# Rotating sixteen rows of each dilated head in one packed tile instead of in two full tiles

## The chip, the cores and the metric

The kernel runs on one core of one Trainium2 chip. The metric is the device time of one execution in microseconds (us), lower is better. A core has five engines that each run their own instruction list in order: PE (TensorE, matrix products and transposes), DVE (VectorE, elementwise work), ACT (ScalarE, activations and copies), POOL (GpSimd) and SP (SyncE, which here issues all transfers). They are tied together by semaphores; data moved by DMA is announced by a semaphore as well.

## The reference

Two layers of an encoder, applied to 256 and 512 tokens (768 together, called T) of width 1024. Each layer adds three things to its input: a mixer with three groups of heads (A dilated, B recurrent, C grouped-query), cross-attention into 256 memory tokens, and a gated feed-forward block with a short convolution. The change touches only the A group, four heads of 64 dimensions whose queries and keys get a rotary embedding in the first 16 of the 64 dimensions:

```python
def rotate(x, cos, sin):
    half = x.shape[-1] // 2
    x1, x2 = x[..., :half], x[..., half:]
    return concatenate([x1 * cos - x2 * sin, x1 * sin + x2 * cos], axis=-1)

def partial_rope(x, rope):            # ROPE_DIMS = 64 // 4 = 16
    return concatenate([rotate(x[..., :16], *rope), x[..., 16:]], axis=-1)
```

The rotated queries and keys then go through a masked attention whose result is the mixture of three (window, dilation) branches. Everything is in 32-bit floats and must come out at that accuracy.

## The kernel before

Activations lie transposed: the feature dimension is on the 128 partitions, the 768 tokens lie along a row. A product of full accuracy is made from halves: each operand is split into a high part and a low remainder (`split`, line 325, one ACT instruction and one DVE instruction), and three matrix products are summed (lines 213 to 215 for projections, 378 and 379 for scores, 400 and 401 for values).

The mixer of a layer is a list of stages, of which two at a time are interleaved by `ahead` (line 353). The call sites are lines 886 to 902: the projection of the first pair of A heads runs beside the second attention of group B (`b_attn(1)`), the projection of the second pair beside the attention of the first pair (`a_attn(0)`). So there are four calls of `a_proj` in the program, two in each layer; they are called places 1 and 2 (layer 0) and places 3 and 4 (layer 1). Nothing is ordered by hand: the tile framework gives each engine its list by priorities and a simulated timeline, so a change of instructions in one stage can shift rows of the stages beside it.

`a_proj` (line 792) projects queries (j=0) and keys (j=1) of two heads into one tile `z2` of 128 partitions by 1536; the two heads stand on partitions 0 to 63 and 64 to 127, so the rows that rotate are partitions 0 to 15 and 64 to 79. POOL clears a second tile `zs2` of the same size (line 798), and four transfers (lines 803 and 804) copy the rows of `z2` into it with their halves swapped. Then three DVE operations run over all 128 partitions for j=0 and three for j=1, `zs*sa`, `z*ca` and `z+zs`; on the rows that don't rotate the tables hold 1 and 0. All elementwise calls go through the helper `tt` (line 158), so they all carry that line. The result is split (the two halves of the queries and of the keys), and `stacks` (line 682) builds from the halves, by transfers of line 365, the operands of the scores: four of 64x768 for the queries, and four of 64x1536 (384 KB) for the keys, called the key stacks below. The score products of the next stage wait for them. Line 943 of the profile of the changed kernel is line 935 here: from line 798 on the numbers shift by up to 8.

Buffers come from two arenas, `arena_f` (plain) and `arena_r` (operands of matrix products); a tile that is freed is handed out again, and whoever gets it waits for the old tile's readers.

Of the kernel before, what the change touches and what calls it, by code (L numbers as in the profile page):

```python
# [13 lines left out]
ALU = mybir.AluOpType  # L14
# [16 lines left out]
T = 768  # L31
# [77 lines left out]
def trunk_kernel(ctx, tc, xT, memT, w_in, w_out, w_xq, w_xkv, w_xo, w_up, w_dn, w_dnt, par, fin_g, cst, fmk, tabs,  # L109
                 out_p, out_s):  # L110
    nc = tc.nc
    V, A, G, PE, SY = nc.vector, nc.scalar, nc.gpsimd, nc.tensor, nc.sync
# [14 lines left out]
    af = Arena(f_all, F_COLS)  # L127
# [3 lines left out]
    ft = lambda n=T: af.tile(n)  # L131
# [25 lines left out]
    def tt(out, a, b, op):  # L157
        V.tensor_tensor(out, a, b, op=op)  # L158
# [81 lines left out]
    def proj(src, xh, xl, evac, streams=STREAMS, sub="", chunks=None):  # L240
        chunks = chunks or wload8(src, sub)
        for c0, n in streams:
            ps = ps_tile(n)
            mm_chunks(ps[:, :n], chunks, xh, xl, c0, n)
            evac(ps[:, :n], c0, n)
# [79 lines left out]
    def split(src, hi, lo, n, scale=None, sub="sp"):  # L325
        hi_op(pick("h" + sub, "A"), hi[:, :n], src[:, :n], scale)
        if scale is None:
            tt(lo[:, :n], src[:, :n], hi.bitcast(F32)[:, :n], ALU.subtract)
        else:
            stt(lo[:, :n], src[:, :n], scale, hi.bitcast(F32)[:, :n], ALU.mult, ALU.subtract)  # L330
# [187 lines left out]
    def mixers(l, xt, x_dram, stats):  # L518
# [7 lines left out]
        def ev_to(z, name):  # L526
            return ev_scaled(z, rbc, name)

        def load_tab(j):
            t = ft()  # L530
            SY.dma_start(out=t, in_=tabs[j])
            return t
# [47 lines left out]
        C = {}  # L580
# [38 lines left out]
        def v_proj(t):  # L619
            zv = ft()  # L620
            proj(w_in[l, t], xh, xl, ev_to(zv, "v%d" % t), sub="w_v%d" % t)
            vv = [rtl(), rtl()]
            v_tokens(zv, 6, [tok(v) for v in vv], "v%d" % t)
            af.free(zv)
            return vv
# [56 lines left out]
        def stacks(qq, kk):  # L682
            out = []
            qf, kf = qq.bitcast(F32), kk.bitcast(F32)
            for e in range(2):
                r = slice(64 * e, 64 * e + 64)
                qs, K = rtl(), rtl(2 * T)
                load_stack(qs, [(0, qf[r, :T]), (64, qf[r, T:])])
                load_stack(K, [(0, kf[r]), (64, kf[r])])
                out.append((qs, K))  # L690
            ar.free(qq, kk)
            return out
# [99 lines left out]
        def a_proj(pg):  # L792
            if pg == 0:
                C["ca"], C["sa"] = load_tab(2), load_tab(3)
                C["fm"] = ft(896)
                SY.dma_start(out=C["fm"], in_=fmk)
            z2, zs2 = ft(2 * T), ft(2 * T)
            G.memset(zs2, 0.0)
            for j in range(2):
                proj(w_in[l, 2 * j + pg], xh, xl, ev_to(z2[:, j * T:(j + 1) * T], "a%d%d" % (pg, j)), sub="w_a%d%d" % (pg, j))  # L800
            for e in range(2):
                r = 64 * e
                SY.dma_start(out=zs2[r:r + 8], in_=z2[r + 8:r + 16])
                SY.dma_start(out=zs2[r + 8:r + 16], in_=z2[r:r + 8])
            parts = []
            for j in range(2):
                z, zs = z2[:, j * T:(j + 1) * T], zs2[:, j * T:(j + 1) * T]
                tt(zs, zs, C["sa"], ALU.mult)
                tt(z, z, C["ca"], ALU.mult)
                tt(z, z, zs, ALU.add)  # L810
                hl = rtl(2 * T)
                if j:
                    split(z, hl[:, :T], hl[:, T:], T, sub="a_sp%d" % pg)
                else:
                    split(z, hl[:, :T], hl[:, T:], T, scale=0.125, sub="saq%d" % pg)
                parts.append(hl)
            af.free(z2, zs2)
            if pg == 1:
                af.free(C["ca"], C["sa"])
            sts = stacks(*parts)  # L820
            return sts, v_proj(4 + pg)
# [65 lines left out]
        sb0 = ahead(lambda: b_proj(0), lambda: c_attn(1, qc1), "1")  # L887
        sb1 = ahead(lambda: b_proj(1), lambda: b_attn(0, sb0), "2")
        sa0 = ahead(lambda: a_proj(0), lambda: b_attn(1, sb1), "3")
        def fa():  # L890
            r = a_proj(1)
            return r
# [421 lines left out]
def _layout(i):  # L1314
# [24 lines left out]
    r = np.arange  # L1339
# [39 lines left out]
    p = np.arange(128)  # L1379
# [31 lines left out]
    both = lambda t: np.concatenate([t[:, :256], t], 1)  # L1411
    tabs[0], tabs[1] = both(np.cos(ang)), both(np.sin(ang))
    inva = (f(500000.0) ** (-np.arange(0, 16, 2, dtype=f) / f(16))).astype(f)
    d = p % 64
    ang = (pos[None].astype(f) * inva[d % 8][:, None]).astype(f)
    tabs[2] = both(np.where((d < 16)[:, None], np.cos(ang), 1))
    tabs[3] = both(np.where((d < 8)[:, None], -np.sin(ang), np.where((d < 16)[:, None], np.sin(ang), 0)))
# [26 lines left out]
```

## Time and profile before

| | us |
|---|---|
| median of 3 runs (2142.23 to 2144.77) | 2144.53 |
| the profiled execution | 2145.01 |
| its span in the trace | 2143.2 |
| PE busy | 2003.8 (93%) |
| DVE busy | 1841.7 (86%) |
| ACT busy | 1061.7 (50%) |
| POOL busy | 7.8 |

PE is busy for 93% of the span. That is an average: in the feed-forward blocks it never idles, in the mixers it does. A row of the timeline names the start, the duration, the engine, the line and the tiles (result first), and in brackets how long the engine stood idle before it and what ended the wait. `SPq` rows are the issuing of transfers. PEclk is the granted TensorE clock as a share of its upper level, so 0.50 is the lower one, 1.2 of 2.4 GHz.

### The profile page before, as it was taken

Reading aid. Unit: us, or ns where it says so; the run is one execution under the profiler, and the core shown is the slowest. Engines: PE = TensorE matmul, PEld = TensorE weight load, DVE = VectorE, ACT = ScalarE, POOL = GpSimd, SP = SyncE. Lnnn points to the kernel's source line nnn. Section 1 sums busy time; section 2 is a strip of 40 time slices with the busy share of each in tenths; the row PEclk is TensorE's granted clock in tenths of the full one; section 3 lists DMA queues with packets and bytes.
Section 4 is the critical chain, followed back from the end, with each engine's and each line's share of the span. In section 5 each row is a group of like instructions: output and inputs, shape, how many; then the busy total and the mean of one; then the engine's idle time right before and its main releaser. Section 6 shows DMA issues by size and latency. Waiting matters only on the chain.

```text
span 2143.2 us, 31059 instructions
## 1 busy us (share of the span) xinstructions
PE 2003.8 (93%) x11280; PEld 1782.8 (83%) x11280; DVE 1841.7 (86%) x3822; ACT 1061.7 (50%) x2119; POOL 7.8 (0%) x32
## 2 busy tenths in 40 slices
PE   7989989998899999999999897999988999999997
PEld 5878768787789999999888775777877999999995
DVE  8787887867999999999977868778779999999998
ACT  4257767547533333333534667565665333333342
POOL 0000000000000000000000000000000000000000
PEclk8989989999999999999999998999999999999998
DMA  5433335342132212212254314343421222222202
GB/s 179 138 82 101 96 89 124 110 132 80 50 90 79 67 62 72 74 63 88 65 179 117 92 44 107 99 111 123 124 64 56 83 70 69 70 69 70 69 30 79
DMA packets 62953, 190.94 MB, mean 89 GB/s; under 512 B 8072, under 2 KB 11400, under 8 KB 62032
## 3 DMA queue, kind: packets, MB, share of 16 engines
q1 hardware_dynamic: 62800, 188.96, 30.1%
q8 instruction: 89, 1.46, 0.3%
q14 instruction: 64, 0.52, 0.1%
HBM read 145.97 MB, written 10.71 MB: 73 GB/s over the span
## 4 chain that ended last, share of the span: by engine, by line
PE 74%; DVE 16%; ACT 4%; DMA 3%; issue 2%; SPq 1%; POOL 0%; DVEq 0%; ACTq 0%
PE rps L1105 8%; PE rps L1107 8%; PE rps L1106 8%; PE rps L1148 5%; PE rps L1149 5%; PE rps L1150 5%; PE prS L213 4%; PE prS L214 4%; PE prS L215 4%; DVE arena_f L158 4%; PE t L392 3%; PE prP L213 2%; PE prP L214 2%; PE prP L215 2%; DVE arena_r L158 2%
## 5 line engine op out<-in xcount | busy, mean ns | idle before, releaser
L158 DVE TENSOR_TENSOR arena_f<-arena_f 128x512 f32<-128x512 f32 (+2 forms) x373 | 265.6, 728 | 27.7 <-DMA arena_f<-arena_f 15.2
L183 ACT CAST wh<-arena_f 128x512 fp32r<-128x512 f32 x266 | 162.2, 621 | 253.0 <-PE rps L1106 212.8
L183 ACT CAST wh<-wr 128x512 fp32r<-128x512 f32 x260 | 159.4, 620 | 236.3 <-PE rps L1106 98.9
L158 DVE TENSOR_TENSOR xall<-rps,xall 128x512 f32<-128x512 f32 (+1 forms) x384 | 197.9, 549 | 14.1 <-PE rps L1150 6.9
L1148 PE MATMUL rps<-arena_r,wh 128*128 128x512 f32 (+1 forms) x608 | 202.6, 339 | 3.4 <-DVE xall L158 3.2
L158 DVE TENSOR_TENSOR wl<-wr,wh 128x512 fp32r<-128x512 f32 x264 | 179.5, 683 | 29.5 <-ACT wh L183 27.9
L1105 PE MATMUL rps<-xha,wh 128*128 128x384 f32 x608 | 203.9, 335 | 0.5 <-ACT wh L183 0.4
L1106 PE MATMUL rps<-xla,wh 128*128 128x384 f32 x608 | 203.4, 335 | 0.0
L1149 PE MATMUL rps<-arena_r,wh 128*128 128x512 f32 (+1 forms) x608 | 201.2, 338 | 0.0
L1107 PE MATMUL rps<-xha,wl 128*128 128x384 f32 x608 | 199.2, 334 | 0.0
L213 PE MATMUL prS<-xha,wh 128*128 128x512 f32 x480 | 188.8, 397 | 3.1 <-DVE arena_f L158 1.0
L215 PE MATMUL prS<-xha,wl 128*128 128x512 f32 x480 | 189.1, 396 | 1.5 <-DVE wl L158 1.5
L214 PE MATMUL prS<-xla,wh 128*128 128x512 f32 x480 | 189.9, 396 | 0.0
L158 DVE TENSOR_TENSOR wl<-arena_f,wh 128x512 fp32r<-128x512 f32 x266 | 179.2, 684 | 1.5 <-ACT wh L183 1.3
L1150 PE MATMUL rps<-arena_r,wl 128*128 128x512 f32 (+1 forms) x608 | 178.3, 339 | 0.0
L158 DVE TENSOR_TENSOR arena_f<-rps,arena_f 128x384 f32<-128x384 f32 x266 | 143.6, 552 | 28.2 <-PE rps L1107 26.0
L1105 PE MATMUL rps<-arena_r,wh 128*128 128x384 f32 x456 | 152.8, 335 | 0.0
L1106 PE MATMUL rps<-arena_r,wh 128*128 128x384 f32 x456 | 152.3, 334 | 0.0
L158 DVE TENSOR_TENSOR arena_r<-t,arena_r 128x512 fp32r<-128x512 f32 x184 | 124.9, 683 | 27.8 <-ACT arena_r L183 24.4
L213 PE MATMUL prP<-xha,wh 128*128 128x256 f32 x480 | 138.9, 289 | 9.8 <-DVE xall L158 5.9
L1107 PE MATMUL rps<-arena_r,wl 128*128 128x384 f32 x456 | 146.4, 334 | 0.0
L392 PE MATMUL t<-cs,arena_f 128*128 128x128 f32 x736 | 125.6, 291 | 13.9 <-DVE arena_r L158 7.5
(235 smaller groups left out, 5004.7 us busy)
## 6 DMA issues: line engine op xcount, KB each, us to landing
arena_f<-in_w_up SPq DMA_DIRECT2D x76, 512.0 KB, 3.6
wr<-in_w_in SPq DMA_DIRECT2D x42, 512.0 KB, 3.6
wr<-in_w_dn SPq DMA_DIRECT2D x40, 512.0 KB, 3.7
wr<-in_w_out SPq DMA_DIRECT2D x32, 512.0 KB, 5.2
arena_r<-arena_r SPq DMA_DIRECT2D x32, 384.0 KB, 6.7
arena_r<-arena_r SPq DMA_DIRECT2D x48, 192.0 KB, 4.0
xall<-in_xT SPq DMA_DIRECT2D x8, 768.0 KB, 8.7
arena_r<-arena_r SPq DMA_DIRECT2D x64, 96.0 KB, 2.2
```

What stands on the lines that cost most here:

```text
L158: V.tensor_tensor(out, a, b, op=op)
L183: A.copy(out, a)
L213: PE.matmul(ps, h[:, j], xh[i][:, c0:c0 + n], start=i == 0, stop=False)
L214: PE.matmul(ps, h[:, j], xl[i][:, c0:c0 + n], start=False, stop=False)
L215: PE.matmul(ps, lo[:, j], xh[i][:, c0:c0 + n], start=False, stop=i == tot - 1)
L392: PE.transpose(t[:, j * n + i * 128:j * n + (i + 1) * 128], ptiles[i][:, (kb + j) * 128:(kb + j + 1) * 128], ident)
L1105: PE.matmul(ps, h[:, k], x[k], start=k == 0, stop=False)
L1106: PE.matmul(ps, h[:, k], x[4 + k], start=False, stop=False)
L1107: PE.matmul(ps, lo[:, k], x[k], start=False, stop=k == 3)
L1148: PE.matmul(ps, h[:, m], hh[i][:, c], start=k == 0 and not tail, stop=False)
L1149: PE.matmul(ps, h[:, m], hlo[i][:, c], start=False, stop=False)
L1150: PE.matmul(ps, lo[:, m], hh[i][:, c], start=False, stop=i == b - 1)
```

## The change

`zs2` goes. Two tiles of 128x768 take its place, `zc` for the rows as they are and `zs` for the rows with their halves swapped. The 16 rotating rows of each of the two heads, of queries and of keys, are packed into four blocks of `zc` and `zs`, at partitions 0, 32, 64 and 96, by 12 transfers (lines 806 to 808). The three DVE operations run once on the packed tiles. Four transfers (line 815) put the rotated rows back into `z2`. The tables repeat every 32 partitions instead of every 64.

```diff
-            z2, zs2 = ft(2 * T), ft(2 * T)
-            G.memset(zs2, 0.0)
+            z2, zc, zs = ft(2 * T), ft(), ft()
+            G.memset(zc, 0.0)
+            G.memset(zs, 0.0)
             for j in range(2):
                 proj(w_in[l, 2 * j + pg], xh, xl, ev_to(z2[:, j * T:(j + 1) * T], "a%d%d" % (pg, j)), sub="w_a%d%d" % (pg, j))
-            for e in range(2):
-                r = 64 * e
-                SY.dma_start(out=zs2[r:r + 8], in_=z2[r + 8:r + 16])
-                SY.dma_start(out=zs2[r + 8:r + 16], in_=z2[r:r + 8])
+            for j in range(2):
+                for e in range(2):
+                    r, b = 64 * e, 64 * j + 32 * e
+                    z = z2[r:r + 16, j * T:(j + 1) * T]
+                    SY.dma_start(out=zc[b:b + 16], in_=z)
+                    SY.dma_start(out=zs[b:b + 8], in_=z[8:16])
+                    SY.dma_start(out=zs[b + 8:b + 16], in_=z[0:8])
+            tt(zs, zs, C["sa"], ALU.mult)
+            tt(zc, zc, C["ca"], ALU.mult)
+            tt(zc, zc, zs, ALU.add)
+            for j in range(2):
+                for e in range(2):
+                    b = 64 * j + 32 * e
+                    SY.dma_start(out=z2[64 * e:64 * e + 16, j * T:(j + 1) * T], in_=zc[b:b + 16])
             parts = []
             for j in range(2):
-                z, zs = z2[:, j * T:(j + 1) * T], zs2[:, j * T:(j + 1) * T]
-                tt(zs, zs, C["sa"], ALU.mult)
-                tt(z, z, C["ca"], ALU.mult)
-                tt(z, z, zs, ALU.add)
+                z = z2[:, j * T:(j + 1) * T]
                 hl = rtl(2 * T)
...
-            af.free(z2, zs2)
+            af.free(z2, zc, zs)
...
-    d = p % 64
+    d = p % 32
```

The lists of the engines move with it, in the mixers of both layers; the feed-forward blocks keep their order. Below are rows of the lists before and after; they tell an order and no times.

DVE at place 3, before. `L769` is the masked softmax work of `b_attn(1)`; `prP` and `prS` rows take the projections out of the accumulators, and the row `x4` is the rotation's first four operations:

```order
2235 L158 TENSOR_TENSOR arena_f<-prP,rbc 128x256
2236 L158 TENSOR_TENSOR wl<-wr,wh 128x512
2237 L158 TENSOR_TENSOR arena_f<-arena_f 128x768 x4
2238 L158 TENSOR_TENSOR xall<-yps,xall 64x512
2239 L769 ISA arena_f,dn<-s,arena_f 128x512
2240 L769 ISA dn 128x1
```

DVE at place 3, after. Row 2210 is the eviction that the last six packing transfers wait for, row 2227 the first of the three rotation operations:

```order
2210 L158 TENSOR_TENSOR arena_f<-prP,rbc 128x256
2211 L158 TENSOR_TENSOR wl<-wr,wh 128x512
2212 L158 TENSOR_TENSOR arena_r<-t,arena_r 128x512 x2
2213 L769 ISA arena_f,dn<-s,arena_f 128x384
2214 L769 ISA dn 128x1
2215 L158 TENSOR_TENSOR arena_f<-prS,rbc 128x512
2216 L158 TENSOR_TENSOR xall<-yps,xall 64x512
2217 L769 ISA arena_f,dn<-s,arena_f 128x384
```

Eight rows further down in the same list the rotation begins:

```order
2225 L769 ISA arena_f,dn<-s,arena_f 128x128
2226 L769 ISA dn 128x1
2227 L158 TENSOR_TENSOR arena_f<-arena_f 128x768
2228 L158 TENSOR_TENSOR arena_r<-t,arena_r 128x512
2229 L769 ISA arena_f,dn<-s,arena_f 128x256
```

The rotation stood right behind the last eviction; now sixteen rows of other work stand between the two.

SP at place 4 (layer 1, second pair), before. The `64x1536` rows are the key stacks, `scr_k` and `scr_v` rows load the operands of the cross-attention:

```order
185 L177 DMA wr<-in_w_out 128x1024
186 L365 DMA arena_r<-arena_r 64x768 x4
187 L365 DMA arena_r<-arena_r 64x1536 x2
188 L365 DMA arena_r<-scr_k 64x2048 x2
189 L365 DMA arena_r<-arena_r 64x1536 x2
190 L935 DMA arena_r<-scr_v 128x1024
```

SP at place 4, after, from the last packing transfer on:

```order
218 L808 DMA arena_f<-arena_f 8x768
219 L815 DMA arena_f<-arena_f 16x768 x4
220 L365 DMA arena_r<-arena_r 64x768 x2
221 L177 DMA wr<-in_w_out 128x1024
222 L365 DMA arena_r<-arena_r 64x768 x2
223 L365 DMA arena_r<-scr_k 64x2048 x2
224 L365 DMA arena_r<-arena_r 64x1536 x4
225 L943 DMA arena_r<-scr_v 128x1024
```

All four key stacks now stand behind the two loads from `scr_k`, where two stood ahead of them. At place 2 one `scr_k` load (512 KB) now stands ahead of the four stacks, where none did.

SP at place 1, after: `L806` to `L808` are the packing transfers, `L815` the way back.

```order
46 L806 DMA arena_f<-arena_f 16x768 x2
47 L177 DMA wr<-in_w_in 128x1024 x2
48 L806 DMA arena_f<-arena_f 16x768
49 L807 DMA arena_f<-arena_f 8x768
50 L808 DMA arena_f<-arena_f 8x768
51 L807 DMA arena_f<-arena_f 8x768
52 L808 DMA arena_f<-arena_f 8x768
53 L807 DMA arena_f<-arena_f 8x768
54 L808 DMA arena_f<-arena_f 8x768
55 L806 DMA arena_f<-arena_f 16x768
56 L807 DMA arena_f<-arena_f 8x768
57 L808 DMA arena_f<-arena_f 8x768
```

Before, the four swaps (two of line 803, two of line 804) stood here; now ten transfers stand behind the last weight loads of this pair, of which the eighth (row 55) completes `zc` and the tenth completes `zs`.

## Rows read from the trace of the kernel before

**Rows 1.** The page: busy times, and the costliest group of DVE.

```profile
PE 2003.8 (93%) x11280; PEld 1782.8 (83%) x11280; DVE 1841.7 (86%) x3822; ACT 1061.7 (50%) x2119; POOL 7.8 (0%) x32
...
L158 DVE TENSOR_TENSOR arena_f<-arena_f 128x512 f32<-128x512 f32 (+2 forms) x373 | 265.6, 728 | 27.7 <-DMA arena_f<-arena_f 15.2
```

**Rows 2.** Windows: both layers' places (first, last) and a feed-forward stretch; first row names columns.

```profile
core 0: us, PE busy (x) PEld busy (x) DVE busy (x) ACT busy (x) POOL busy (x), PEclk, DMA share, GB/s
300.00:400.00 100.00, 92.97 (x531) 77.32 (x529) 85.30 (x248) 70.65 (x169) 1.38 (x1) 0.97 0.45 113
700.00:1000.00 300.00, 300.00 (x1724) 286.13 (x1723) 286.03 (x484) 112.29 (x171) 0.00 (x0) 1.00 0.22 69
1300.00:1400.00 100.00, 85.04 (x444) 68.94 (x443) 75.17 (x265) 60.32 (x150) 2.77 (x2) 0.86 0.40 105
```

**Rows 3.** Timeline of DVE: the rotation at places 1 to 4.

```profile
300.79 3.56 DVE L158 TENSOR_TENSOR arena_f<-arena_f 128x768 f32<-128x768 f32 x4 [1.98 <-DMA arena_f<-arena_f]
...
346.44 3.57 DVE L158 TENSOR_TENSOR arena_f<-arena_f 128x768 f32<-128x768 f32 x4 [4.20 <-DMA arena_f<-arena_f]
...
1349.90 3.56 DVE L158 TENSOR_TENSOR arena_f<-arena_f 128x768 f32<-128x768 f32 x4 [4.63 <-DMA arena_f<-arena_f]
...
1395.70 3.56 DVE L158 TENSOR_TENSOR arena_f<-arena_f 128x768 f32<-128x768 f32 x4 [4.41 <-DMA arena_f<-arena_f]
...
1400.71 0.94 DVE L158 TENSOR_TENSOR arena_f<-arena_f 128x768 f32<-128x768 f32 x1
```

**Rows 4.** Timeline of SP: first and last of four swapping transfers at place 1; first at place 3.

```profile
295.70 0.73 SPq L803 DMA_DIRECT2D arena_f<-arena_f  x1
...
297.90 0.62 SPq L804 DMA_DIRECT2D arena_f<-arena_f  x1
...
1344.74 0.72 SPq L803 DMA_DIRECT2D arena_f<-arena_f  x1
```

**Rows 5.** Windows: the stretches behind places 1 and 3.

```profile
315.00:320.00 5.00, 1.70 (x5) 0.95 (x6) 5.00 (x26) 3.78 (x12) 0.00 (x0) 0.77 0.72 160
320.00:325.00 5.00, 4.70 (x18) 3.42 (x17) 5.00 (x32) 5.00 (x15) 0.00 (x0) 0.54 0.86 198
...
1365.00:1370.00 5.00, 2.19 (x8) 1.00 (x6) 5.00 (x25) 4.21 (x13) 0.00 (x0) 0.91 0.89 186
1370.00:1375.00 5.00, 4.89 (x18) 3.90 (x17) 5.00 (x31) 4.66 (x14) 0.00 (x0) 0.50 0.63 153
```

**Rows 6.** Timeline of PE: its longest wait behind place 1.

```profile
317.07 0.47 PE L378 MATMUL s<-arena_r 128*128 128x512 f32 x1 [2.14 <-DVE dn L158]
```

**Rows 7.** Timeline of PE: the waits for the key stacks, places 2 and 4.

```profile
365.99 0.47 PE L378 MATMUL s<-arena_r 128*128 128x512 f32 x1 [1.45 <-DMA arena_r<-arena_r]
...
1427.05 0.74 PE L378 MATMUL s<-arena_r 128*128 128x512 f32 x1 [2.69 <-DMA arena_r<-arena_r]
```

**Rows 8.** Chain of waits: from the last issue of swaps at place 1, of stacks later.

```profile
297.90 2.81 DMA arena_f<-arena_f
...
359.87 5.98 DMA arena_r<-arena_r
...
1417.60 9.21 DMA arena_r<-arena_r
```

**Rows 9.** Windows: the transfers at place 2, and the low clock at place 4.

```profile
355.00:360.00 5.00, 5.00 (x29) 4.21 (x28) 4.97 (x11) 4.95 (x11) 0.00 (x0) 1.00 0.89 240
360.00:365.00 5.00, 4.54 (x29) 3.81 (x27) 4.17 (x10) 3.11 (x8) 0.00 (x0) 1.00 0.94 198
...
1425.00:1430.00 5.00, 2.95 (x9) 2.50 (x10) 2.07 (x5) 2.68 (x6) 0.00 (x0) 0.71 0.40 122
```

**Rows 10.** Timeline of DVE: the two splits of place 2 (DVE's part of each).

```profile
356.29 0.95 DVE L161 SCALAR_TENSOR_TENSOR arena_r<-arena_f,arena_r 128x768 fp32r<-128x768 f32 x1
...
358.38 0.95 DVE L158 TENSOR_TENSOR arena_r<-arena_f,arena_r 128x768 fp32r<-128x768 f32 x1
```

## The prediction

> **What bounds the kernel now.** I read the page first, then the windows, then the timeline of each engine at the four places, then the chain of waits. The page says PE 93% busy and DVE 86%, and its costliest group of DVE, the arena operations, has 27.7 us of idle time before it, of which 15.2 us end with a transfer within the arena [rows 1]. The windows show that 93% is an average of two regimes: in a feed-forward stretch PE is busy for 300.00 of 300 us with DVE at 286.03, while around the A heads of layer 0 PE has 92.97 of 100 and in layer 1 85.04 of 100, and the clock there is below the upper level for part of the time [rows 2]. So only the mixers have something to give.
>
> The 15.2 us are the four waits for the swapping transfers: 1.98, 4.20, 4.63 and 4.41 us [rows 3]. They are DVE's idle time, not PE's. PE's losses lie elsewhere, in two forms. Behind places 1 and 3 DVE has a backlog, is 100% busy for ten microseconds, and PE starves: it is busy for 1.70 and 2.19 of 5 us, and in the five that follow it runs at a granted clock of 0.54 and 0.50, that is near or at the 1.2 GHz level, after having stood idle [rows 5]; its longest single wait there, 2.14 us, ends with DVE [rows 6]. At places 2 and 4 PE waits 1.45 and 2.69 us for the key stacks [rows 7].
>
> **The change part by part.**
>
> *Removed.* Three of six DVE operations per place. Four in a row take 3.56 us, 0.89 each; single ones 0.94 [rows 3]. So 2.7 us per place, 10.7 in all. POOL clears the same number of bytes; POOL is hardly used.
>
> *Added on SP.* 16 transfers per place instead of four. Issuing one takes 0.62 to 0.73 us [rows 4], I take 0.68, and from the last issue to DVE's start it is 2.9 us (297.90 to 300.79, rows 3 and 4; the chain books 2.81 of it as the transfer, rows 8). Before, the chain is 5.1 us (295.70 to 300.79). With k transfers left after the last eviction it is (k-1) x 0.68 + 2.9.
>
> The Trainium skill, in "DMA: Bandwidth & Descriptors", section "Rules for kernel authors", speaks against the change: it says to merge small transfers, since below 64 KB one pays mostly overhead; the change cuts 48 KB swaps into pieces of 24 and 48 KB. Its section "Anatomy of one DMA" (fitted for another issuing path) gives about 2 us plus the bytes at 436 GB/s, an estimate of 2.1 us for 48 KB; the chain of waits shows 2.81, and the trace decides. With 2.1 the sum would come out about 1.4 us lower per place, for the two hops.
>
> *Added hop.* The split waits for rotated rows that come back by DMA: 0.68 + 2.9 = 3.6 us from the last operation for the queries, 3 x 0.68 + 2.9 = 4.9 for the keys. Whatever is queued behind the waiting row on DVE waits too: the softmax of the B heads and the evictions that PE's next products need.
>
> *Place 1.* The first operation needs the eighth transfer after the eviction: 7 x 0.68 + 2.9 = 7.7 us. In the new order some 20 rows stand in between, about 4.2 us by their like in the trace (five of 128x512 at 0.73, the page's group mean, rows 1; the others short); the wait is 3.5 us against 1.98, so +1.5. Three operations go, -2.7. The hop of 3.6 us is covered by about 2.8 us, +0.8. DVE comes out 0.4 us ahead. I take 0. From below, the most that can come back is what PE loses there: 3.3 + 0.3 us idle, and 4.70 x 0.46 + 1.70 x 0.23 = 2.6 us of clock [rows 5], 6.2. From above, with the cover late as well, 1.5 + 2.8 = 4.3 us.
>
> *Place 3.* All twelve stand behind the last eviction: 11 x 0.68 + 2.9 = 10.4 us. Sixteen rows stand in between, about 5.5 us by the same means; the wait of 4.9 us is nearly the 4.63 of before, but 5.5 us of softmax and evictions have run in the meantime instead of adding to the backlog. The hop is covered by about 4 us of rows; the splits themselves come later than before, by 1 to 3 us, since more work stands ahead of them. I take -2, most of what the removed operations give. Bounds: -5.5 (idle 2.8 + 0.1, clock 4.89 x 0.50 + 2.19 x 0.09 = 2.6, rows 5) and +4 (the hop uncovered).
>
> *Place 2.* Six transfers follow the eviction: 6.3 us, 1.2 more than before, and 2.5 us of softmax now stands in the gap that was 4.20 us. Before, the splits started 9.85 and 11.94 us after the rotation did [rows 3, 10]. Now: rotation 1.2 later, three operations instead of six, then about 6 us of other rows that hide the 4.9 us hop; the splits come out 1 to 2 us earlier. Against it stands one more 512 KB load ahead of the stacks; at the 198 to 240 GB/s of that stretch [rows 9] it takes 2.2 to 2.6 us. The stacks land 1 us later; PE already waits for them, so +1. Bounds: -1.45 (the wait of rows 7 gone) and +3.
>
> *Place 4.* The first six transfers run during the second projection, six follow: 6.3 us. There DVE has the slack to hide the hop. Before, the last two stacks were issued at 1417.60 - 0.5, long after the split, and took 9.21 us [rows 8]; now all four can go as soon as the splits are done, but behind 1 MB. The total in flight is the same, the issue a little sooner: -1. Bounds: -3.6 (2.69 of wait, rows 7, and 2.95 x 0.29 = 0.9 of clock, rows 9) and +4.7 (1 MB at 222 GB/s ahead of the first stack).
>
> Sum: 0 - 2 + 1 - 1 = -2. The profiled execution took 2145.01 us, 1.8 more than its span, and lies 0.48 above the median; 2144.53 - 2 = 2142.5. The bounds add to -16.8 and +16, but they are four places that need not fall the same way, so the forecast's own range is about 2138 to 2147. The saving of 10.7 us is thus mostly not seen: DVE either waits longer for transfers or was not what PE waited for.
>
> **The rivals.**
>
> *A: the backlog closes.* With the softmax moved into the waits, DVE is 5 us ahead where PE starves, PE no longer stands idle, and its clock stays at the upper level. For it: the clock fell in the very stretches after the wait [rows 5], so a short gain on DVE counts twice. Against it: between PE's waits stands ACT as well, 5.00 of 5 us busy in 320 to 325 [rows 5]. Two thirds of 6.2 + 5.5 give -8: about 2136.5.
>
> *B: the key stacks come late.* The second hop and the loads from `scr_k` ahead of the stacks push the stacks back at places 2 and 4, where PE waits for nothing else: 2.4 us at place 2, up to 4.7 at place 4, and a longer wait of PE is followed by the lower clock as the 2.69 us one was [rows 7, 9]. It decides as soon as the stacks at place 4 land later than 2 us after the time of before. About 2144.5 + 6 = 2150.5, slower.
>
> *C: the neighbours decide.* The lists of the mixers of both layers are rearranged beyond the rotation, the recurrent stage of layer 1 most of all; that may cost or give 5 us without a link to the rotated rows. 2139 or 2149, either way alike.
>
> *D: the transfers run one after another.* If each of the 12 more had to land before the next, a place would pay 12 x 2.8 = 34 us, less 5 of cover: 2144.5 + 4 x 29 = 2260. The rows speak against it: four issues 0.7 us apart, and DVE starts 2.9 us after the last [rows 3, 4]. The Trainium skill's rule in the same section that transfers to separate partition halves serialize points this way; the rows of place 1 don't show it for these sizes.
>
> That the change doesn't do what it says is ruled out by the order: three rotation rows per place instead of six, and 64 transfers.
>
> **How the numbers follow.** No change is told from a measurement at about 0.2% here, 4.3 us: faster is below 2140.2, slower above 2148.8. Forecast 0.43, of which 0.12 falls below 2140.2; A 0.24; B 0.23; C 0.09, half each; D 0.01. Faster 0.12 + 0.24 + 0.04 = 0.40; slower 0.23 + 0.04 + 0.01 = 0.28; same 0.32, which is the rest of the forecast's and a bit of C's. The range takes in A and B with their spread: 2131 to 2154.
>
> **What would show it.** On DVE: three operations of 0.9 us per place, a wait before the first of about 3.5 us at place 1 and 4 to 5 at place 3, and no wait above 1.5 us before a split. On SP: issues of 0.6 to 0.7 us, the splits of place 2 1 to 2 us sooner after the last eviction. On PE: at places 2 and 4 a wait of 1 to 3 us for the stacks; behind 1 and 3 still a stretch at the lower clock. If that stretch is gone, A holds; if the wait at place 4 is above 4 us, B. The forecast is wrong if the spans before and after the A heads differ by more than 3 us, for then C decides.

## The result, and the profile after

The changed kernel takes 2154.34 us (median of 6 runs, 2151.16 to 2159.85), the kernel before on the same chip 2144.11 us. The ratio is 1.0058, 95% interval 1.0043 to 1.0073: 0.6% slower, which is 10.2 us by the medians and 12.4 us by the ratio. Predicted were 2142.5 us and a range of 2131 to 2154.

The page of the changed kernel, the lines that answer to [rows 1]:

```profile
PE 2002.4 (93%) x11280; PEld 1785.4 (83%) x11280; DVE 1837.9 (85%) x3810; ACT 1063.3 (49%) x2119; POOL 8.4 (0%) x36
...
L158 DVE TENSOR_TENSOR arena_f<-arena_f 128x512 f32<-128x512 f32 (+2 forms) x361 | 255.5, 722 | 10.6 <-ACT arena_f L557 3.4
```

On DVE the change did what it says: 12 operations fewer, 10.1 us less work in the group, and its idle time down from 27.7 to 10.6 us. The busy time of PE is as before, so in sum the loss is new idle time of PE: 150.2 us of the span (2152.6 less 2002.4) where it was 139.4. The windows that answer to [rows 2], with two more (columns as there):

```profile
300.00:400.00 100.00, 88.09 (x502) 74.64 (x501) 75.00 (x209) 68.59 (x165) 1.42 (x2) 0.93 0.50 121
700.00:1000.00 300.00, 300.00 (x1726) 286.36 (x1725) 286.08 (x484) 112.66 (x171) 0.00 (x0) 1.00 0.22 69
1300.00:1400.00 100.00, 84.22 (x429) 66.63 (x428) 78.89 (x283) 69.56 (x173) 2.96 (x4) 0.88 0.42 108
360.00:380.00 20.00, 15.33 (x72) 12.26 (x71) 9.95 (x26) 11.12 (x29) 0.00 (x0) 0.83 0.82 188
...
560.00:600.00 40.00, 28.54 (x142) 24.38 (x142) 29.09 (x76) 17.08 (x37) 0.00 (x0) 0.83 0.15 50
```

The same two late windows of the kernel before:

```profile
360.00:380.00 20.00, 18.55 (x109) 15.33 (x108) 16.29 (x46) 16.31 (x43) 0.00 (x0) 1.00 0.87 217
560.00:600.00 40.00, 34.97 (x199) 30.52 (x199) 37.65 (x89) 17.74 (x33) 0.00 (x0) 0.91 0.20 61
```

Two stretches lose: place 2 (360 to 380) and one of which the prediction does not speak at all, the end of the cross-attention and the start of the first feed-forward block (560 to 600). In both PE has more idle time than before, and the granted clock is lower: 0.83 where it was 1.00 and 0.91. The second comparison holds when the windows are moved along with the work, which is 6 us late there: 566 to 606 of the changed kernel has PE busy for 30.65 us at 0.83.

To see where a trace gains or loses, each DVE and ACT instruction outside the rotation is looked up in both traces. The lag below is its end in the other trace less its end in the kernel before, in us, the median over those that end within 20 us from the time at the head of the column (in the kernel before). The experiments are named in the next section. At 240 no list differs from that of the kernel before, yet the lags already run from -0.3 to -3.0: so much do two executions differ. Only the growth along a row tells something.

```
                       240    480    540   1000   1180   1480   2100
changed kernel        -0.3    5.7    6.0   14.3   13.0    9.6    9.8
e1                    -3.0    8.1    9.1    9.0    6.7   13.0   13.2
e2                    -1.3   13.3   11.9   15.8   15.8    6.1    7.8
e3                    -2.2   14.7   13.7   16.0   14.6    8.0    7.0
e4                    -1.7   -2.0   -2.3   -0.4   -1.9  -10.4   -7.7
e5                    -2.2   -0.3    1.0    1.1   -0.2   -0.5    1.7
e6                    -2.0   -2.7   -2.0    6.4    4.9   -2.5    0.9
e9                    -2.3   -2.3   -2.3    4.4    4.5   -2.4   -0.5
e13                   -1.6    1.3    2.7    6.1    4.8   -1.7   -0.2
```

Between 240 and 480 lie places 1 and 2, between 540 and 1000 the start of the feed-forward block, between 1180 and 1480 the mixer of layer 1 with places 3 and 4. The changed kernel loses 6 us in the first, 8 in the second, and gets 3.5 back in the third.

DVE's timeline, the rotation at places 1 to 4, and the two splits of place 2 (answering to [rows 3, 10]):

```profile
303.00 0.96 DVE L158 TENSOR_TENSOR arena_f<-arena_f 128x768 f32<-128x768 f32 x1 [1.23 <-DMA arena_f<-arena_f]
...
347.04 2.82 DVE L158 TENSOR_TENSOR arena_f<-arena_f 128x768 f32<-128x768 f32 x3 [0.81 <-DMA arena_f<-arena_f]
...
355.48 0.96 DVE L161 SCALAR_TENSOR_TENSOR arena_r<-arena_f,arena_r 128x768 fp32r<-128x768 f32 x1
...
357.29 0.96 DVE L158 TENSOR_TENSOR arena_r<-arena_f,arena_r 128x768 fp32r<-128x768 f32 x1
...
1361.10 0.96 DVE L158 TENSOR_TENSOR arena_f<-arena_f 128x768 f32<-128x768 f32 x1
...
1408.78 0.96 DVE L158 TENSOR_TENSOR arena_f<-arena_f 128x768 f32<-128x768 f32 x1 [0.29 <-DMA arena_f<-arena_f]
```

The four waits of 1.98 to 4.63 us became 1.23, 0.81, 0 and 0.29 (the last before the second operation of place 4). The splits of place 2 come 0.8 and 1.1 us sooner than in [rows 10]. The transfers that put the rows back are hidden as well: over the whole run they end one wait of 0.5 us on DVE and one of 0.5 us on ACT (line 815). PE's timeline at places 2 and 4 (answering to [rows 7]):

```profile
370.94 0.80 PE L378 MATMUL s<-arena_r 128*128 128x512 f32 x1 [4.67 <-DMA arena_r<-arena_r]
...
1433.16 0.77 PE L378 MATMUL s<-arena_r 128*128 128x512 f32 x1 [6.17 <-DMA arena_r<-arena_r]
```

The waits for the key stacks grew from 1.45 and 2.69 us. And SP's timeline at place 2 says what stands ahead of those stacks (line 365 issues stacks, and the loads of `scr_k` of the cross-attention):

```profile
349.89 2.43 SPq L815 DMA_DIRECT2D arena_f<-arena_f  x4
354.17 0.33 SPq L943 DMA_DIRECT2D arena_r<-scr_v  x1
354.91 1.15 SPq L365 DMA_DIRECT2D arena_r<-arena_r  x2
356.10 0.61 SPq L365 DMA_DIRECT2D arena_r<-scr_k  x1
356.81 1.24 SPq L365 DMA_DIRECT2D arena_r<-arena_r  x2
358.15 1.07 SPq L177 DMA_DIRECT2D wr<-in_w_out  x1
359.32 5.22 SPq L365 DMA_DIRECT2D arena_r<-arena_r  x4
```

and the same stretch of the kernel before, where these loads come behind the stacks:

```profile
354.17 1.16 SPq L365 DMA_DIRECT2D arena_r<-arena_r  x2
355.47 0.48 SPq L177 DMA_DIRECT2D wr<-in_w_out  x1
357.27 7.26 SPq L365 DMA_DIRECT2D arena_r<-arena_r  x6
364.98 2.95 SPq L365 DMA_DIRECT2D arena_r<-scr_k  x2
367.97 1.74 SPq L935 DMA_DIRECT2D arena_r<-scr_v  x2
```

Two loads of 512 KB, one of `scr_v` and one of `scr_k`, now stand ahead of the key stacks. They are for the cross-attention, whose first exponential runs at 487 us. The section on the change and the prediction name only the `scr_k` load.

### The profile page after: what moved, and what is told of

It reads as the page before. It is cut to its first block, busy times and chain, and to the rows that moved or that the text cites. A ratio compares the mean times of both kernels' runs of the same rounds, so it can differ in the third digit from the quotient of the medians.

```text
span 2152.6 us, 31131 instructions
## 1 busy us (share of the span) xinstructions
PE 2002.4 (93%) x11280; PEld 1785.4 (83%) x11280; DVE 1837.9 (85%) x3810; ACT 1063.3 (49%) x2119; POOL 8.4 (0%) x36
## 4 chain that ended last, share of the span: by engine, by line
PE 73%; DVE 15%; ACT 4%; DMA 4%; issue 2%; SPq 1%; DVEq 0%; ACTq 0%
PE rps L1113 8%; PE rps L1115 8%; PE rps L1114 8%; PE rps L1156 5%; PE rps L1157 5%; PE rps L1158 5%; PE prS L213 4%; PE prS L214 4%; PE prS L215 4%; DVE arena_f L158 4%; PE prP L213 2%; PE t L392 2%; PE prP L214 2%; PE prP L215 2%; DVE arena_r L158 2%
## 5 line engine op out<-in xcount | busy, mean ns | idle before, releaser
L158 DVE TENSOR_TENSOR arena_f<-arena_f 128x512 f32<-128x512 f32 (+2 forms) x361 | 255.5, 722 | 10.6 <-ACT arena_f L557 3.4
L214 PE MATMUL prP<-xla,wh 128*128 128x256 f32 x480 | 138.0, 287 | 0.0
```

Source lines behind the costliest of these rows:

```text
L214: PE.matmul(ps, h[:, j], xl[i][:, c0:c0 + n], start=False, stop=False)
```

## The experiments

The runs came in five groups, each with its own runs of the kernel before beside it (medians from 2140.8 to 2144.1 us). Kernels of different groups are compared by their ratios to it, times 2142 us; intervals are of 95%. A difference by the ratios and one by the medians can be 2 us apart.

Theory: the packing hides its own transfers, and the 10 us come from the new order of the other work. Rival: the second hop (the four transfers that put the rows back) makes the stacks late by itself.

### e1 and e5: the packed rotation in the old order

Every instruction outside the rotation is tied to the one that precedes it on its engine in the kernel before. The two packing tiles are cut from one allocation, so that all other operands keep their addresses. A table at the head of the file shifts the line numbers shown by 125: line 310 there is 185 here (ACT's part of the split), 475 is 350 (copies of the values), 503 is 378, 889 is 764.

```
-            z2, zc, zs = ft(2 * T), ft(), ft()
+            z2, zz = ft(2 * T), ft(2 * T)
+            zc, zs = zz[:, :T], zz[:, T:]
...
+            for a, b in zip(q, q[1:]):
+                tc.add_manual_dep(at[b], at[a].name, info, reason="pin")
```

> The packed rotation, with every instruction outside the rotation held in the order that the kernel before has on its engine, and with the two packing tiles cut from one allocation, so that every other operand lies at the address it had before. Theory (the 10 us come from the new order of the other work: cross-attention loads ahead of the stacks, and a reordered start of the feed-forward): about 2141 us (2136 to 2147), since the packing hides its own transfers and the DVE saves its idle time. Rival 1 (the second hop of the packing makes the key stacks late by itself): at least 2149 us, with matmuls that wait 4 us or more for a stack at places 2 and 4. Rival 2 (a pinned order is worse because it fits another timing): above 2155 us.

Measured: 2159.11 us, ratio 1.0081 [1.0066, 1.0097]. The theory fails here: in the old order the packing costs 16.5 us by the medians. The first rival's sign, a wait of PE of 4 us or more for a stack, isn't seen either: the longest is 3.1 us, at place 4. e5 is the same without the put-back transfers.

```
-                        SY.dma_start(out=z2[64 * e:64 * e + 16, j * T:(j + 1) * T], in_=zc[b:b + 16])
```

> The packed rotation in the old order, as in the first run of this study, but the four transfers that put the rotated rows back are left out, so the splits take rows that were not rotated and the output is another. Theory (the second hop: the ACT's split of the queries starts 2 to 4 us later than in the kernel before, and all that is queued behind it on the ACT with it): the loss of 11 us between 300 and 400 us of the span and that of 4 us in the second layer go, 2137 to 2146 us. Rival (the loss is the wait for both halves before the first rotation, or the packing transfers themselves): 2152 to 2160 us.

Measured: 2143.21 us, ratio 1.0009 [0.9997, 1.0021]. So in that order the second hop is the whole loss, 15.4 us by the ratios, and the rest of the packing is worth nothing, though DVE has 12 operations less. The order is tied down in e5 too, so the tying is not what costs (the second rival of e1). ACT's timeline of e1 shows how:

```profile
309.56 0.51 ACT L889 ACTIVATE arena_f<-arena_f,colm 128x256 f32<-128x256 f32 x1 [9.05 <-DMA arena_f<-arena_f]
...
357.49 0.84 ACT L310 ACTIVATE arena_r<-arena_f 128x768 fp32r<-128x768 f32 x1 [1.62 <-DMA arena_f<-arena_f]
...
369.55 0.37 ACT L475 CAST arena_r<-vps 128x256 fp32r<-128x256 f32 x1 [4.53 <-DMA arena_r<-arena_r]
```

At place 1 ACT stands for 9.05 us before an exponential of the B heads. In the kernel before and in e5 it waits there as well, but less, and for DVE:

```profile
307.05 0.51 ACT L764 ACTIVATE arena_f<-arena_f,colm 128x256 f32<-128x256 f32 x1 [3.26 <-DVE arena_f L158]
...
306.88 0.51 ACT L889 ACTIVATE arena_f<-arena_f,colm 128x256 f32<-128x256 f32 x1 [4.63 <-DVE arena_f L283]
```

The exponential has nothing to do with the rotation, but it writes columns 1536 to 1791 of `arena_f`, which the tile of the swapped rows has in the kernel before, and `zc` here. In the kernel before that tile is free when DVE has read it; `zc` is read by the put-back transfers, and its next owner waits for them. Two rows behind it on ACT comes the split of the queries, which needs the put-back rows themselves, so how much of the wait is due to the columns alone no run shows. At place 2 ACT stands before the split, and then before a copy of values that waits for the stacks (4.53 us; 3.29 in e5, 1.83 in the kernel before). PE follows. Its timeline in e1, where the longest wait of [rows 6] was 2.14 us:

```profile
316.12 0.76 PE L503 MATMUL s<-arena_r 128*128 128x512 f32 x1 [5.58 <-DVE dn L283]
...
321.94 0.66 PE L471 MATMUL vps<-cs,arena_f 128*128 128x128 f32 x2 [4.64 <-DVE arena_r L283]
```

Only the first of the two is the hop's: in e5 it is 1.17 us, while the second is there with 5.14.

The window around places 1 and 2 in e1:

```profile
300.00:400.00 100.00, 82.73 (x458) 69.32 (x457) 69.21 (x211) 62.00 (x150) 1.42 (x2) 0.90 0.48 116
```

The same window in e5, where PE is busy for 7 us more and the clock is back at 0.97 [rows 2]:

```profile
300.00:400.00 100.00, 89.72 (x517) 75.21 (x516) 78.98 (x237) 67.92 (x165) 1.42 (x2) 0.97 0.47 115
```

Everything behind the waiting row on ACT waits with it. The Trainium skill, "Perfetto Trace Analysis", section "Per-engine timelines", under the TensorE instruction, says that "ACT/DVE/GPSIMD are strict FIFO"; the trace agrees, for no row of ACT's list runs in the 9.05 us.

### e2 and e3: a new order with the packing, and without it

e2 is the changed kernel with the one allocation of e1 and its order planned anew. e3 is the kernel before, old rotation and all, tied to the order of e2.

> The packed rotation with the two packing tiles cut from one allocation of the size of the old one: every operand outside the rotation then lies at the address of the kernel before, and only the order is planned anew. At place 2 one half MB load of cross-attention values and two quarter MB loads of its keys still stand ahead of the last stacks. Theory (order decides, not addresses): 2150 to 2158 us, a wait of 3 to 6 us for a stack at place 2. Rival (the changed addresses of the split allocation decide): 2140 to 2146 us.

> The kernel before, its rotation untouched, with every instruction outside the rotation held in the order that the packed kernel of one allocation (the run beside this one) has on its engine; all operands lie where they lay before. Theory (order decides): as slow as that run within 4 us, 2149 to 2160 us, though nothing is packed. Rival (the second hop decides): 2141 to 2147 us, like the kernel before.

Measured: e2 2151.26 us, ratio 1.0036 [1.0023, 1.0049]; e3 2156.31 us, 1.0061 [1.0047, 1.0076]. These two are of one group: in e2's order the packed rotation is the faster by 5 us (the intervals just meet), in the old order the slower by 16. Of these two orders, each suits the rotation with which it was planned. The stack wait of e2's expectation doesn't show on PE, whose longest wait between 280 and 480 is one of 7.4 us for DVE; and the key loads that it gives as a quarter MB are of 512 KB each on the page. What the packing is worth can therefore not be said without its order.

### e4, e7 and e8: nothing changed but the plan

The planner simulates the program, and a memset cut in two changes what it does with hundreds of other instructions. e4 is the kernel before, e7 is e2 with one memset in place of two, e8 the changed kernel with four.

```
-            G.memset(zs2, 0.0)
+            G.memset(zs2[:, :T], 0.0)
+            G.memset(zs2[:, T:], 0.0)
```

> The kernel before with its one memset of the swap tile made in two halves: as good as nothing changes in the work, but the order is planned anew, and about 600 instructions of the 7,000 or so in the two mixer stages stand elsewhere in their queues. Theory (the planned order alone moves the time by several us): off the kernel before by 2 to 10 us, in either direction. Rival (order is worth nothing): within 2 us of it, 2142 to 2146 us.

> The packed kernel of one allocation with one memset in place of two: nothing changes in the work, the order is planned anew. If the planned order moves the time by up to 10 us whatever the change, 2138 to 2160 us and off its sister of two memsets (2151 us) by 3 us or more; if the packing decides, 2149 to 2154 us.

> The packed kernel with its two memsets made in two halves each: nothing changes in the work, the order is planned anew, and some 1,000 instructions stand elsewhere. If the planned order moves the time by up to 10 us whatever the change, 2143 to 2160 us and off the packed kernel (2154 us) by 3 us or more; if the packing decides, 2152 to 2157 us, with the 7 us at the start of the first feed-forward block still in it.

Measured: e4 2133.56 us, ratio 0.9960 [0.9947, 0.9972]; e7 2140.95 us, 1.0001 [0.9992, 1.0011]; e8 2152.34 us, 1.0050 [1.0037, 1.0063]. POOL's 8 us of memsets are not on anyone's path (in the kernel before nothing waits for line 798), yet e4 gains 9 us and e7 is 7.5 us faster than e2 (by the ratios). e8 came out like the changed kernel, within 3 us of it and so against the theory; it has the same two losses in its trace (7 us each by the lag). A new plan alone moves this kernel by 7 to 9 us, nearly as much as the result itself. So the next runs look for single causes within a plan.

### e6: the cross-attention loads behind the stacks

```
+            with tc.issue_after(lk):
+                SY.dma_start(out=vt.bitcast(F32), in_=scr_v[l, j])
+                load_stack(K, [(0, src), (64, src)])
```

`lk` is the last key stack. Up to the end of the heads of layer 0 PE, DVE and ACT keep the order of the changed kernel.

> The packed kernel, with the loads of cross-attention keys and values held on SP behind the last stack of place 2 and of place 4; in the first layer nothing else moves on PE, DVE or ACT up to the end of the heads. Theory of the prediction's price (the loads ahead of the stacks cost the 4 to 5 us at place 2): the wait of PE for the stack at place 2 falls from 4.67 us to 2 us or less, that at place 4 from 6.17 us to 3 us or less, and the time to 2145 to 2150 us. Rival (the loads only fill time in which the queue waits for the put-back rows): 2152 to 2157 us, the stack wait gone or not.

Measured: 2146.92 us, ratio 1.0036 [1.0022, 1.0050]: 4.7 us less than the changed kernel by the ratios; than e8, its like in the same group, 5.4 us less by the medians and 3.0 by the ratios. PE's timeline at place 2 (line 379 there is 378 here):

```profile
366.05 0.47 PE L379 MATMUL s<-arena_r 128*128 128x512 f32 x1 [1.49 <-DMA arena_r<-arena_r]
```

and the window that lost most:

```profile
360.00:380.00 20.00, 18.51 (x107) 15.51 (x106) 14.81 (x39) 16.09 (x40) 0.00 (x0) 1.00 0.85 218
```

The wait is 1.49 us where it was 4.67, and the clock 1.00 where it was 0.83; both are as before the change. At place 4 the wait falls from 6.17 to 2.48 us. In the table of lags the loss between 240 and 480 is gone: the lag goes from -2.0 to -2.7, where the changed kernel goes from -0.3 to 5.7. The 8 us between 540 and 1000 are still there.

### e9 and e13: the addresses at the start of the feed-forward block

Cutting the second tile into two allocations changes the order in which the arena hands out columns, up to the end of the layer. In the changed kernel the last norm before the first feed-forward block puts one of its squares on columns 3840 to 4095 of `arena_f`; in the kernel before it doesn't. The block's first evacuation of 512 columns writes 3840 to 4351. ACT's timeline in the kernel before, that evacuation (from `prS`) and the one of 256 columns (from `prP`):

```profile
556.28 0.58 ACT L1060 COPY arena_f<-prS 64x512 f32<-64x512 f32 x1
...
568.27 0.37 ACT L1060 COPY arena_f<-prP 64x256 f32<-64x256 f32 x1
```

and in the changed kernel, with the rows of DVE (the first of the two operations is the last reader of that square) and PE:

```profile
578.72 0.37 ACT L1068 COPY arena_f<-prP 64x256 f32<-64x256 f32 x1 [0.44 <-DVE arena_f L158]
...
581.80 1.02 DVE L158 TENSOR_TENSOR arena_f<-arena_f 128x256 f32<-128x256 f32 x2
...
583.30 0.58 ACT L1068 COPY arena_f<-prS 64x512 f32<-64x512 f32 x1
...
584.53 0.50 PE L213 MATMUL prS<-xha,wh 128*128 128x512 f32 x1 [1.83 <-ACT arena_f L1069]
```

The evacuation comes 27 us later, and its PSUM buffer, one of two, is held until then; PE waits for it. ACT doesn't stand idle before it: the plan has put it behind the evacuation from `prP`, ahead of which it stood before. So the feed-forward block does not keep its order at its start, contrary to the section on the change. The wait shown on PE is 1.83 us of some 8 that are lost; the rest is spread over that stretch and was not followed row by row. e9 gives the kernel before the same addresses without any packing (and eight swap transfers in place of four):

```
-            z2, zs2 = ft(2 * T), ft(2 * T)
+            z2, zc, zs = ft(2 * T), ft(), ft()
...
+                for j, h in enumerate((zc, zs)):
```

> The old rotation, nothing packed, but its second tile cut into two allocations of half the size, one for each half of the rows (so eight short swap transfers in place of four): from there on nearly all operands lie where the packed kernel has them. Theory (in the packed kernel the start of the first feed-forward block is late by the addresses: the first evacuation there lands on columns that the last square of the norm before still holds): the lag behind the kernel before grows by 6 to 9 us between 540 and 600 us of the span here too, and the time is that of the run with the memset in halves (2133.6 us) plus as much, 2139 to 2150 us. Rival (the packing's delays do it): the lag grows by less than 3 us there, 2131 to 2137 us.

Measured: 2148.19 us (2140.81 to 2153.94), ratio 1.0031 [1.0016, 1.0045]. The lag grows from -2.3 to 4.4 between 540 and 1000, with the old rotation. ACT's row in e9:

```profile
573.49 0.58 ACT L1063 COPY arena_f<-prS 64x512 f32<-64x512 f32 x1 [0.31 <-DVE arena_f L158]
```

e13 goes the other way: e6, with the 16 tiles of that norm put where the kernel before has them.

```
+PLACES = {
+    "on": False,
+    512: [12800, 8704, 3072, 13312, 1024, 0, 512, 1536],
+    256: [10752, 11008, 2048, 2304, 5632, 5888, 9216, 9472],
+}
...
+        if PLACES.get(n) and PLACES["on"]:
+            return self.cut(PLACES[n].pop(0), n, fl)
```

> The packed kernel with the cross-attention loads behind the last stacks (2146.9 us, as run before) and the 16 tiles of the last norm ahead of the first feed-forward block put at the addresses that the kernel before gives them; the packing and its allocation stay. Theory (the late start of that block comes from those addresses): the lag behind the kernel before grows by less than 3 us between 540 and 600 us of the span in place of 8.5, so that it is 0 or less at 1000 us; the second layer is planned anew, which may move the end by some us, 2135 to 2144 us. Rival (the late start comes with the packing in another way): the lag is still 5 us or more at 1000 us, 2144 to 2150 us.

Measured: 2137.45 us (2134.44 to 2144.31), ratio 0.9977 [0.9965, 0.9989]: 0.2% faster than the kernel before, and by the ratios 12.6 us less than e6. ACT's row of the evacuation (lines are shifted by 14 and more by the table of places):

```profile
559.39 0.58 ACT L1084 COPY arena_f<-prS 64x512 f32<-64x512 f32 x1 [0.26 <-PE prS L227]
```

It is back in its place, and now ends a wait for PE, not for an address. The trace shows less than the median: the lag still grows by 3.4 us (2.7 to 6.1) where e6 has 8.4, and it is not 0 at 1000, so the expectation holds for the time and the evacuation but not for the lag. That trace is of the slowest of 12 runs, and the second layer was planned anew as well; about 5 us are shown at the place itself (8.4 less 3.4), and how the rest divides is not settled.

### e10, e11, e12 and e14: bounds

e10 and e11 are e7 and e4 with the loads late; e12 is the kernel before in its own order without any rotation (its memset is still there); e14 is e10 in its own order without the second hop.

> The packed kernel of one allocation and one memset (2140.95 us) with the cross-attention loads behind the last stacks; PE, DVE and ACT keep their order, only SP's changes. Theory (the loads cost only where PE then waits for a stack, which it does for 3.5 us in the second layer there): 2136 to 2141 us. Rival (loads that move back are missed in the cross-attention): 2143 to 2148 us.

> The kernel before with its memset in halves (2133.6 us) and the cross-attention loads behind the last stacks: the candidate for the fastest version. Theory: the wait for stacks in the second layer, 3.7 us, falls to 2 us or less, 2130 to 2134 us. Rival (the loads are missed later): 2136 us or more.

> The kernel before without any rotation of the dilated heads (no swap transfers, no memset, none of its 24 DVE instructions; the splits take the rows as they come, so the output is another), every other instruction held in the old order. It bounds what any cheaper rotation can give in this order. Theory (the rotation is hidden, its DVE time off the path): 2134 to 2142 us, a gain of at most 6 us. Rival (the 23 us of DVE work on the path): 2118 to 2132 us.

> The packed kernel of one allocation, one memset and late loads (2138.8 us), every instruction held in the order that it has there, but without the four transfers that put the rotated rows back, so that the splits take rows that were not rotated and the output is another. Theory (an order that was planned with the second hop hides most of it): a gain of 1 to 6 us, 2133 to 2138 us. Rival (the second hop costs the same 16 us in any order): 2120 to 2128 us.

Measured: e10 2138.80 us, ratio 0.9986 [0.9976, 0.9996], 3 us less than e7 by the ratios, with intervals that overlap; e11 2134.76 us, 0.9965 [0.9952, 0.9979], no gain over e4, between its theory and its rival (its waits for stacks in the second layer fell from 3.7 to 2.7 us, not to 2); e12 2136.44 us, 0.9972 [0.9961, 0.9984]; e14 2137.98 us, 0.9973 [0.9962, 0.9984].

e12 is the ceiling in the old order: with no rotation at all, 24 DVE operations and four waits gone, 6 us come back. e14 prices the second hop in an order planned with it: 0.0013 of 2142, 2.8 us, with intervals that overlap, so it is not clear of zero; against 0.0072, 15.4 us, in the old order. The same transfers, the same sizes.

The fastest version is e4, the old rotation with its memset in halves: 2133.56 us, below both kernels.

## Why the prediction was wrong

**What held.** The removed DVE operations, the issue times on SP (0.5 to 0.7 us), hidden put-backs, splits at place 2 about 1 us sooner, and that DVE's saving is mostly not seen: all as said. The waits before the rotation were forecast too long, 3.5 to 5 us where 0 to 1.2 came. Rival D is out. One reading was loose: 0.73 us is a mean over several shapes, a 128x512 row alone takes 0.68, which moves the sum of place 1 by 0.2 us.

Rival A did not come at either place. The stretch at the lower clock behind place 1 is still there, and the one behind place 3 has moved with the rotation, which starts 11 us later (1361.10 in place of 1349.90). The windows of the changed kernel that answer to [rows 5]:

```profile
315.00:320.00 5.00, 1.70 (x5) 0.93 (x4) 4.13 (x10) 5.00 (x13) 0.00 (x0) 0.71 0.67 174
320.00:325.00 5.00, 5.00 (x21) 4.10 (x20) 4.62 (x23) 2.94 (x9) 1.42 (x2) 0.60 1.00 220
...
1375.00:1380.00 5.00, 2.20 (x6) 0.93 (x4) 4.40 (x15) 5.00 (x15) 0.74 (x1) 0.53 0.51 102
1380.00:1385.00 5.00, 5.00 (x19) 4.33 (x20) 5.00 (x19) 2.57 (x7) 0.74 (x1) 0.50 0.93 216
```

DVE is no longer 100% busy in three of the four, and PE is busy for 1.70 and 2.20 of 5 us all the same.

**The terms of the mixers.** Between the places the rows stand in another order, so a lag says little there; the places are taken two by two. Places 1 and 2 (240 to 480), forecast 0 and +1: the lag grows by 6.0 us in the changed kernel, and by -0.7 in e6, where the loads don't stand in the way. The mixer of layer 1 with places 3 and 4 (1180 to 1480), forecast -3: -3.4 in the changed kernel, -7.4 in e6. That is no proof of these two terms: e9, which packs nothing, has -6.9 there, and e4 -8.5. So the sizes that the packing by itself was given are not contradicted, and not shown either.

**The step that failed first** is the term of place 2, "Against it stands one more 512 KB load ahead of the stacks", so "+1", and with it the -1 of place 4. Places 1 and 2 cost 6.0 us in the changed kernel where the sum has +1. Two things were mis-sized. At place 2 it is two loads, 1 MB, since the `scr_v` load ahead of them was passed over, and PE's wait for the stacks grew by 3.2 us (1.45 to 4.67). And the lower clock after the longer wait was left out of the term, though it stood in rival B: 15.33 us of work at 0.83 in 360 to 380 make 2.6 us (15.33 x 0.17), an estimate from that window. The two make 5.8. At place 4 the wait grew from 2.69 to 6.17 us, and e6, planned anew in that layer, gains 4.0 us more there than the changed kernel. B's price of 6 us was about right (4.7 by e6), its sign for place 4 ("above 4 us") came with 6.17, and it had 0.23 where the SP order already held what decides it.

**The step that failed second** is "So only the mixers have something to give": the sum has no term for what follows the heads. The second loss lies there, 8.3 us by the lag from 540 to 1000. The nearest thing to it is rival C, "the neighbours decide", 0.09, half each way, but C too speaks of the lists of the mixers only, while a changed allocation moves addresses to the end of the layer. The cause stands in the two programs before any run: a square of the norm on columns that the next block writes first, and ACT's list of that block in another order. The prediction's own sign for C, spans before and after the A heads that differ by more than 3 us, came.

A third thing the prediction didn't have, and which the changed kernel's plan mostly avoids: a tile that transfers read back is free later. The longest wait of e1 shown above, 9.05 us, ends with such transfers; e5, without them, has 4.63 there.

Together, by the ratios: +12.4 us for the changed kernel, less 4.7 (e6), less 12.6 (e13, its new plan included), leaves -4.9. With both causes out the packed kernel is 5 us below the one before, where the forecast had 2. That agreement is not worth much: e4 is 8.6 us below it with a new plan and nothing else.

**What stays open.** Why e4 gains 8 us in the mixer of layer 1, why e7's plan lacks e2's loss at places 1 and 2, and the 3 to 4 us that the changed kernel gets back in layer 1 between 1180 and 1300, ahead of place 3, were not traced to single instructions. Nor were e9's runs explained, which lie between 2141 and 2154.

## What to carry to other kernels

Where a planner sets the order, a change is measured together with a new plan, and here a new plan alone was worth 7 to 9 us: make the same comparison with a change that does nothing, and tie the order down to see what the change itself costs. Read the order of the queues beyond the changed lines, count every byte that now stands ahead of what someone waits for, and price the lower clock after the wait with it. Keep the sizes of allocations when a tile is cut up; another hand-out order can put a late tile under an early writer some two hundred microseconds further on.

## What was not expected of the hardware

The second hop, four transfers of 48 KB at each place, cost 15.4 us in one order, and in another 2.8 us, which is not clear of zero. The Trainium skill, "DMA: Bandwidth & Descriptors", section "Rules for kernel authors", says that under 64 KB one pays mostly overhead. The trace agrees: 48 KB took 2.81 us [rows 8], where 198 to 240 GB/s [rows 9] would make some 0.2 us, an estimate. But the transfers are the same in both orders, with 0.54 us in the median for one issue in the changed kernel (line 815, 16 issues). What differs is the order of the other instructions, and with it what is queued behind the one that waits. Without the rotation (e12) DVE loses 24 operations of 0.9 us, some 21 us, and the kernel gains 6.
